# Sum of squares of an input tile in halves on ACT and DVE, and the softmax's maximum with its sign turned

## The chip, the core and the metric

The program runs on one core of a Trainium2 chip. The metric is the device time of one execution in microseconds; three executions of the kernel before gave 641.45, 641.72 and 641.73, a median of 641.72. The profile of a kernel is taken from one execution of its own. The engines are named as in the profile: PE multiplies matrices, PEld loads its weights, ACT applies functions, DVE is the vector engine, POOL the general engine, SP issues DMAs.

## The reference, cut to what matters

One layer of a decoder: a normalized input is projected, three groups of heads mix it (a recurrent one, one with block-sparse attention, a gated one), and a feed-forward block follows. The change touches the first normalization and the attention's softmax:

```python
def rmsnorm(x, g):                       # x: 512 tokens of 1024 channels
    y = x * lax.rsqrt(jnp.mean(x * x, axis=-1, keepdims=True) + 1e-6)
    return y * g
...
logits = einsum(q, k) * 0.125            # 6 heads of 64 channels, 512 tokens
p = softmax(where(mask, logits, -inf), axis=-1)
o = einsum(p, v)
```

## The kernel before

Tokens lie in four tiles of 128. `xt` holds the input as four tiles of 128 partitions (tokens) by 1024 channels. All matrix products use a split of each operand into a rounded high part and a low remainder (h and l in the names), so each product is three.

The first stage, up to about 25 us, has its order written out by hand on all five engines: what stands first in the program runs first on its engine. `norm_x(t)` takes the sum of squares of tile t on ACT (L265, with an accumulator output into `ss`), then forms the mean plus 1e-6 on POOL (L266) and its power of -1/2 on POOL (L267, into `rs`). For tiles 0 and 1 `diag_x` (L288, DVE) turns `rs` into a diagonal matrix by which PE turns and scales at once; for tiles 2 and 3 `scale_x` (L270, DVE) multiplies the tile and PE transposes it. `turn_x(th, k)` transposes channel block k of a pair of tiles on PE, and gives its high part on ACT (L281, `bigh`) and its low part on DVE (L282, `bigl`). `split` cuts the first weights: the high part on ACT (L296), the low part on POOL (L297). On DVE the order of the first stage is: diag of tile 0, the copy of the norm's gain `gcol` (L311), diag of tile 1, then the L282 of the channel blocks 0 to 7 and the two L270. `norm_x(2)` and `norm_x(3)` stand behind `turn_x(0, 5)` and `turn_x(0, 6)`. PE alternates between high and low products of a block as `turn_x` delivers it.

Behind this stage PE's order is still given by the program (the class `Order` interleaves side work by due times that are counted in PE's columns), while the order on ACT, DVE, POOL and SP is made by a planner that simulates the program and picks by priority what is ready. POOL's preparations (masks, constants) are such work, and the planner has put them ahead of the first L266.

The attention's `scores(qb)` has PE multiply queries `qs` and keys into a PSUM bank `s`, DVE take the maximum of a row (L845), DVE multiply it by -0.125 (L846), ACT take exp(0.125 s + that) with its sum (L848), DVE the reciprocal (L849) and the scaling of the row (L850). This happens 24 times, between 141 and 226 us. `turned(qb)` then transposes the row on PE (L117) and copies it on ACT (L859). `dense_qk` produces the queries: the high part of the product by a copy on ACT (L987), the low part by a difference on DVE (L989).

Of the kernel before, what the change touches and what calls it, by code (L numbers as in the profile page):

```python
# [8 lines left out]
F32 = mybir.dt.float32  # L9
F32R = mybir.dt.float32r  # L10
BF = mybir.dt.bfloat16
AF = mybir.ActivationFunctionType
OP = mybir.AluOpType
AX = mybir.AxisListType

S = 512
D = 1024
# [79 lines left out]
def block_kernel(ctx: ExitStack, tc: tile.TileContext, x, pre_mix_g, w_in, rwkv_mu, rwkv_w0, rwkv_w2,  # L97
# [4 lines left out]
    act, dve, pool, sp = nc.scalar, nc.vector, nc.gpsimd, nc.sync  # L102
# [34 lines left out]
    def sb():  # L137
        return bank("sb", 3)

    def ob():  # L140
        return bank("ob", 1)
# [4 lines left out]
    def ct(shape, name, dt=F32):  # L146
        return const.tile(shape, dt, name=name)
# [78 lines left out]
    ss = ct([128, 4], "ss")  # L226
    rs = ct([128, 4], "rs")
# [11 lines left out]
    xt = p0p.tile([128, NB, D], F32, name="xt")  # L239
    junk = p0p.tile([128, D], BF, name="junk")  # L240
    diag = p0p.tile([128, 2, 128], F32, name="diag")
    ET = mybir.EngineType
    with tc.manual_schedule(engines={ET.PE, ET.Activation, ET.DVE, ET.Pool, ET.SP}):
# [18 lines left out]
        pe.transpose(pc, grow0, ident[:KB, :KB])  # L262

        def norm_x(t):
            act.activation(junk, xt[:, t, :], AF.Square, scale=1.0 / 32, accum_out=ss[:, t:t + 1])  # L265
            pool.tensor_scalar(rs[:, t:t + 1], ss[:, t:t + 1], 1.0, 1e-6, op0=OP.mult, op1=OP.add)  # L266
            pool.tensor_tensor(rs[:, t:t + 1], rs[:, t:t + 1], mhalf[:, 0:1], op=OP.pow)  # L267

        def scale_x(t):
# [35 lines left out]
        def step(i, th, k):  # L305
            dense(i, th, wh, h1, k)
            dense(i, th, wh, l1, k)

        norm_x(0)
        diag_x(0)  # L310
        dve.tensor_copy(gcol, pc)  # L311
        norm_x(1)
        diag_x(1)
        split(0, 0, pool)
# [4 lines left out]
        for k in range(KB):  # L319
            dense(0, 0, wh, h1, k)  # L320
            if k == 0:
                split(1, 0, pool)
            if k == 2:
                split(1, 1, pool)
            if k < KB - 3:
                turn_x(0, k + 3)
            if k in (2, 3):
                norm_x(2 + (k > 2))
            if k in (4, 6):
                scale_x(k // 2)  # L330
            dense(0, 0, wh, l1, k)
            if k >= LAG:
                step(1, 0, k - LAG)
# [133 lines left out]
    def dense_fm(free=False):  # L467

        wh, wl = feed.next()
        wh = wh.rearrange("p (k c) -> p k c", k=KB)  # L470
        wl = wl.rearrange("p (k c) -> p k c", k=KB)
        p = acc()
        for k in range(KB):
            pe.matmul(p, wh[:, k], h1[:, k], start=(k == 0), stop=False)
            pe.matmul(p, wh[:, k], l1[:, k], start=False, stop=False)
            pe.matmul(p, wl[:, k], h1[:, k], start=False, stop=(k == KB - 1))
            if free:
                od.signal("free%d" % k)
            if k < KB - 1:
                od.pump()  # L480
        return p
# [28 lines left out]
    HR = [slice(0, 64), slice(64, 128)]  # L510
# [318 lines left out]
    def head(pair, hh):  # L829
        yield "qk%d" % pair  # L830
        yield "inverse"
        yield "vt"
        if pair:
            yield "att%d" % (pair - 1)
        a = 2 * pair + hh

        def scores(qb):
            n = 128 * qb + 128
            s = sb()
            qs, ks, kl = QK[pair]  # L840
            pe.matmul(s[:, :n], qs[:, hh, n - 128:n], ks[:, hh, :n], start=True, stop=False, skip_group_check=True)
            pe.matmul(s[:, :n], qs[:, hh, n - 128:n], kl[:, hh, :n], start=False, stop=False, skip_group_check=True)
            pe.matmul(s[:, n - 128:n], identb, negm, start=False, stop=True, skip_group_check=True)
            mx = att.tile([128, 4], F32, name="mx%d" % hh, bufs=2)
            dve.tensor_reduce(mx[:, 0:1], s[:, :n], axis=AX.X, op=OP.max)  # L845
            dve.tensor_scalar(mx[:, 1:2], mx[:, 0:1], -0.125, None, op0=OP.mult)  # L846
            e = st_["at2"].tile([128, S], F32, name="ee%d" % hh, bufs=2)
            act.activation(e[:, :n], s[:, :n], AF.Exp, bias=mx[:, 1:2], scale=0.125, accum_out=mx[:, 2:3])  # L848
            dve.reciprocal(mx[:, 3:4], mx[:, 2:3])  # L849
            dve.tensor_scalar(e[:, :n], e[:, :n], mx[:, 3:4], None, op0=OP.mult)  # L850
            return e

        def turned(qb, e):
            n = 128 * qb + 128
            pt = sb()
            for kb in range(qb + 1):
                pe.transpose(pt[:, 128 * kb:128 * kb + 128], e[:, 128 * kb:128 * kb + 128], ident)
            pts = st_["at2"].tile([128, NB, 128], F32, name="pts%d" % hh, bufs=2 - hh)
            act.copy(pts[:, :qb + 1, :], pt[:, :n].rearrange("p (k c) -> p k c", c=128))  # L859
            return pts  # L860

        def weighted(qb):

            n = 128 * qb + 128
            if pair not in pos:
                pos[pair] = ob()
            for kb in range(qb + 1):
                for h in range(2):
                    pe.matmul(pos[pair][HR[h], n - 128:n], vt[:, kb, pair, h, :], ptss[pair, h, qb][:, kb, :],
                              start=(qb == 0), stop=(kb == qb), skip_group_check=True)  # L870
            od.signal("sum%d_%d" % (pair, qb))

        yield 1500.0 * hh
        e = scores(0)
        due = od.t + T_SM + 2.4 * 128
        for qb in range(NB):
            yield due - od.t
            if not hh and qb > 1:
                yield "sum%d_%d" % (pair, qb - 2)
            ptss[pair, hh, qb] = turned(qb, e)  # L880
            t0 = od.t
            if qb < NB - 1:
                e = scores(qb + 1)
                due = od.t + T_SM + 2.4 * (128 * qb + 256)
            od.signal("pts%d_%d" % (a, qb), t0 + T_PT + 0.8 * (128 * qb + 128) - od.t)
            if hh:
                yield "pts%d_%d" % (a - 1, qb)
                yield "pts%d_%d" % (a, qb)
                weighted(qb)
        od.signal("head%d" % a)  # L890
# [90 lines left out]
    def dense_qk(b):  # L981

        qs, ks, kl = QK[b]
        p = dense_fm()
        with tc.high_priority(offset=PRI_W):
            for h in range(2):
                act.copy(qs[HR[h], h], p[HR[h]])  # L987
            for h in range(2):
                dve.tensor_tensor(qs[HR[1 - h], h], p[HR[h]], qs[HR[h], h].bitcast(F32), op=OP.subtract)  # L989
        od.pump()  # L990
        for h in range(2):
            pool.memset(kl[HR[1 - h], h].bitcast(F32), 0.0)
        p = dense_fm()
        with tc.high_priority(offset=PRI_W):
            for h in range(2):
                act.copy(ks[HR[h], h], p[HR[h]])
            for h in range(2):
                dve.tensor_tensor(kl[HR[h], h], p[HR[h]], ks[HR[h], h].bitcast(F32), op=OP.subtract)
        for h in range(2):
            pool.tensor_scalar(ks[HR[1 - h], h], ks[HR[h], h].bitcast(F32), 1.0, 0.0, op0=OP.mult, op1=OP.add)  # L1000
        od.pump()
        od.signal("qk%d" % b, T_QK)
# [8 lines left out]
    AO = [ca.rearrange("p a b -> p (a b)")[:, :S], ca.rearrange("p a b -> p (a b)")[:, S:],  # L1011
          ar[:, 0, 0:4].rearrange("p c a s -> p (c a s)")]
    dense_qk(0)
    dense_qk(1)
    dense_qk(2)
    p = dense_fm()
    shift(p, 10, sg)
# [21 lines left out]
    for b in range(2):  # L1039
        p = dense_fm(b == 1)  # L1040
# [574 lines left out]
```

## Time and profile before

| | us |
|---|---|
| median of three executions (lowest, highest) | 641.72 (641.45, 641.73) |
| the profiled execution's own time | 641.61 |
| its span in the trace | 639.9 |
| PE busy in the span | 623.0 |
| DVE busy | 490.1 |
| ACT busy | 327.7 |
| POOL busy | 56.8 |

The span is 1.7 us shorter than the execution's time; what lies around it is no part of the trace. Matrix products run one into the other, and a busy PE is not a PE at its peak; but an idle PE is time in which it waited.

### The profile page before, as it was taken

The page shows a single profiled execution, that of the slowest core. Times are in us where ns is not written, and L with a number is a line of the kernel's source. Part 1 is how long each engine was busy: PE and PEld are TensorE (multiplying, and loading weights), DVE is VectorE, ACT ScalarE, POOL GpSimd, SP SyncE. Part 2 cuts the span into 40 slices and gives each one's busy share as a digit, 9 for nine tenths or more (in the row PEclk, how much of TensorE's full clock was granted, in tenths as well). Part 3 has the DMA queues.
Part 4 walks back from the last instruction along what each step waited for, and adds up shares of the span by engine and source line. Part 5 has one row for each costly group of instructions (what it writes and reads, how often), then busy time and mean ns, then how long its engine had stood idle before and what let it go on. Part 6 is the DMA issues. An engine that isn't in the chain of part 4 may idle for free.

```text
span 639.9 us, 11545 instructions
## 1 busy us (share of the span) xinstructions
PE 623.0 (97%) x4582; PEld 548.6 (86%) x4582; DVE 490.1 (77%) x835; ACT 327.7 (51%) x582; POOL 56.8 (9%) x107
## 2 busy tenths in 40 slices
PE   7999999999999999999999999999999999999995
PEld 7877778877767887888999999999999988888884
DVE  2789969886575779558988888788897748979825
ACT  6653543365554464447755555555455434646511
POOL 7021111032130100011000000000000000000001
PEclk9999999999999999999999999999999999999999
DMA  7421111421211117315424333343333235775403
GB/s 233 125 64 50 57 50 61 129 69 47 59 34 34 35 40 289 122 44 155 139 73 130 99 107 101 92 131 99 100 104 96 67 122 198 256 232 182 160 0 132
DMA packets 84981, 69.12 MB, mean 108 GB/s; under 512 B 2968, under 2 KB 70976, under 8 KB 84928
## 3 DMA queue, kind: packets, MB, share of 16 engines
q1 hardware_dynamic: 83024, 65.76, 33.1%
q10 hardware_dynamic: 1904, 2.63, 1.4%
q8 instruction: 36, 0.59, 0.4%
q14 instruction: 17, 0.14, 0.1%
HBM read 66.28 MB, written 2.10 MB: 107 GB/s over the span
## 4 chain that ended last, share of the span: by engine, by line
PE 79%; DVE 4%; issue 1%; ACT 1%; POOL 0%; DVEq 0%; POOLq 0%; ACTq 0%
PE acc L112 34%; PE sb L112 30%; PE rb L112 5%; PE yb L112 5%; PE ob L112 3%; PE sb L117 2%; DVE wl L185 1%; DVE x L1566 1%; ACT wdad L1532 0%; DVE tinv L657 0%; PE rb L117 0%; PE yb L117 0%; DVE y L666 0%; POOL rs L1564 0%; DVE s L1556 0%
## 5 line engine op out<-in xcount | busy, mean ns | idle before, releaser
L112 PE MATMUL acc<-bigh,wh 128*128 128x512 f32 (+1 forms) x168 | 67.2, 403 | 0.3 <-ACT bigh L281 0.3
L112 PE MATMUL acc<-bigl,wh 128*128 128x512 f32 (+1 forms) x168 | 63.3, 381 | 0.3
L183 ACT ACTIVATE wh<-wf 128x512 fp32r<-128x512 f32 (+2 forms) x60 | 40.4, 711 | 44.2 <-PE acc L112 29.3
L112 PE MATMUL sb<-h,wh 128*128 128x256 f32 x260 | 61.4, 282 | 0.0
L112 PE MATMUL sb<-l,wh 128*128 128x256 f32 x260 | 61.4, 282 | 0.0
L185 DVE TENSOR_TENSOR wl<-wf,wh 128x512 fp32r<-128x512 f32 (+2 forms) x60 | 47.0, 805 | 17.5 <-ACT wh L183 15.4
L112 PE MATMUL acc<-bigh,wl 128*128 128x512 f32 (+1 forms) x168 | 59.0, 376 | 0.0
L1318 ACT ACTIVATE wh<-wf 128x1024 fp32r<-128x1024 f32 x38 | 39.9, 1058 | 30.6 <-DVE wf L1339 13.8
L1319 DVE TENSOR_TENSOR wl<-wf,wh 128x1024 fp32r<-128x1024 f32 x38 | 46.0, 1222 | 10.4 <-ACT wh L1318 10.3
L112 PEld LDWEIGHTS sb<-l,wh 128*128 128x128 f32 x260 | 47.5, 190 | 0.0
L112 PEld LDWEIGHTS sb<-h,wh 128*128 128x128 f32 x260 | 47.5, 190 | 0.0
L1411 ACT ACTIVATE wh<-wf 128x1024 fp32r<-128x1024 f32 x25 | 26.2, 1058 | 33.5 <-PE sb L112 23.4
L112 PE MATMUL sb<-h,wl 128*128 128x256 f32 x260 | 41.0, 282 | 0.0
L1412 DVE TENSOR_TENSOR wl<-wf,wh 128x1024 fp32r<-128x1024 f32 x25 | 30.1, 1220 | 10.6 <-ACT wh L1411 10.6
L112 PEld LDWEIGHTS acc<-bigh,wh 128*128 128x128 f32 x168 | 31.8, 189 | 7.0 <-issue 1.3
L112 PEld LDWEIGHTS acc<-bigl,wh 128*128 128x128 f32 x168 | 31.8, 189 | 5.6 <-DVE bigl L282 0.9
L1318 ACT ACTIVATE wh<-sums 128x1024 fp32r<-128x1024 f32 x19 | 20.1, 1061 | 30.3 <-PE acc L112 17.2
L112 PEld LDWEIGHTS sb<-h,wl 128*128 128x128 f32 x260 | 35.4, 191 | 0.0
L112 PEld LDWEIGHTS acc<-bigh,wl 128*128 128x128 f32 x168 | 29.8, 188 | 6.2
L1319 DVE TENSOR_TENSOR wl<-sums,wh 128x1024 fp32r<-128x1024 f32 x19 | 23.2, 1223 | 11.7 <-ACT wh L1318 11.7
L1564 POOL TENSOR_TENSOR rs<-rs,mhalf 128x1 f32<-128x1 f32 x4 | 2.2, 550 | 333.3 <-DVE rs L1559 329.9
L1357 DVE TENSOR_TENSOR frow<-sb,grow 128x512 f32<-128x512 f32 x19 | 13.1, 688 | 17.2 <-PE sb L112 17.2
(489 smaller groups left out, 1764.3 us busy)
## 6 DMA issues: line engine op xcount, KB each, us to landing
wf<-in_w_ffn_in_dram SPq DMA_DIRECT2D x76, 256.0 KB
wf<-in_w_ffn_out_dram SPq DMA_DIRECT2D x37, 512.0 KB
wf<-in_w_in_dram SPq DMA_DIRECT2D x21, 512.0 KB
wf<-in_w_out_dram SPq DMA_DIRECT2D x8, 512.0 KB
wf<-in_w_ffn_in_dram SPq DMA_DIRECT2D x6, 512.0 KB
xt<-in_x_dram SPq DMA_DIRECT2D x4, 512.0 KB
x<-in_x_dram SPq DMA_DIRECT2D x4, 512.0 KB
out_dram<-x SPq DMA_DIRECT2D x8, 256.0 KB
```

The lines of the kernel that those rows point to most:

```text
L112: return nc.tensor.matmul(out_, lhsT, rhs, **kw)
L117: return nc.tensor.transpose(out_, in_, idn)
L183: act.activation(h[:, c], t[:, c], AF.Copy)
L185: eng.tensor_tensor(l[:, c], t[:, c], h[:, c].bitcast(F32), op=OP.subtract)
L1318: act.activation(h, src, AF.Copy)
L1319: dve.tensor_tensor(l, src, h.bitcast(F32), op=OP.subtract)
L1357: dve.tensor_tensor(em[1], pc, su.rearrange("p i c -> p (i c)"), op=OP.add)
L1411: act.activation(h, src, AF.Copy)
L1412: dve.tensor_tensor(l, src, h.bitcast(F32), op=OP.subtract)
L1564: pool.tensor_tensor(r, r, mhalf[:, 0:1], op=OP.pow)
L1566: dve.scalar_tensor_tensor(x2[:, t, c], src, r, x2[:, t, c], op0=OP.mult, op1=OP.add)
```

## The change

Each of the four L265 takes 512 of the 1024 channels on ACT; the other 512 are squared and summed on DVE by one instruction with an accumulator output (the mean's factor 1/1024 goes into it), and a second DVE instruction on one column adds the two halves and 1e-6. POOL's L266 goes; L267 stays. In the softmax the maximum is taken with its sign turned by the same instruction, L846 goes, and the factor 0.125 moves from the exponential into both parts of the queries.

```diff
         def norm_x(t):
-            act.activation(junk, xt[:, t, :], AF.Square, scale=1.0 / 32, accum_out=ss[:, t:t + 1])
-            pool.tensor_scalar(rs[:, t:t + 1], ss[:, t:t + 1], 1.0, 1e-6, op0=OP.mult, op1=OP.add)
+            act.activation(junk[:, 0:512], xt[:, t, 0:512], AF.Square, scale=1.0 / 32, accum_out=ss[:, t:t + 1])
+            dve.scalar_tensor_tensor(junk[:, 512:], xt[:, t, 512:], 1.0 / D, xt[:, t, 512:], op0=OP.mult, op1=OP.mult,
+                                     accum_out=rs[:, t:t + 1])
+            dve.scalar_tensor_tensor(rs[:, t:t + 1], ss[:, t:t + 1], 1e-6, rs[:, t:t + 1], op0=OP.add, op1=OP.add)
             pool.tensor_tensor(rs[:, t:t + 1], rs[:, t:t + 1], mhalf[:, 0:1], op=OP.pow)
...
-            dve.tensor_reduce(mx[:, 0:1], s[:, :n], axis=AX.X, op=OP.max)
-            dve.tensor_scalar(mx[:, 1:2], mx[:, 0:1], -0.125, None, op0=OP.mult)
+            dve.tensor_reduce(mx[:, 1:2], s[:, :n], axis=AX.X, op=OP.max, negate=True)
             e = st_["at2"].tile([128, S], F32, name="ee%d" % hh, bufs=2)
-            act.activation(e[:, :n], s[:, :n], AF.Exp, bias=mx[:, 1:2], scale=0.125, accum_out=mx[:, 2:3])
+            act.activation(e[:, :n], s[:, :n], AF.Exp, bias=mx[:, 1:2], accum_out=mx[:, 2:3])
...
             for h in range(2):
-                act.copy(qs[HR[h], h], p[HR[h]])
+                act.activation(qs[HR[h], h], p[HR[h]], AF.Copy, scale=0.125)
             for h in range(2):
-                dve.tensor_tensor(qs[HR[1 - h], h], p[HR[h]], qs[HR[h], h].bitcast(F32), op=OP.subtract)
+                dve.scalar_tensor_tensor(qs[HR[1 - h], h], p[HR[h]], 0.125, qs[HR[h], h].bitcast(F32),
+                                         op0=OP.mult, op1=OP.subtract)
```

## Rows read from the trace of the kernel before

**Rows 1.** Stretches: us, then busy us (instructions) of PE, PEld, DVE, ACT, POOL; clock, DMA

```profile
17.00:30.00 13.00, 12.98 (x95) 11.87 (x95) 9.19 (x22) 8.63 (x17) 0.89 (x6) 1.00 0.37 104
141.00:225.00 84.00, 81.51 (x886) 63.33 (x881) 53.49 (x155) 43.56 (x118) 14.44 (x18) 1.00 0.15 42
```

**Rows 2.** Timeline, 4 to 9 us: start, duration, instruction, [idle before <-releaser]

```profile
4.70 1.06 ACT L265 ACTIVATE junk<-xt 128x1024 bf16<-128x1024 f32 x1 [1.77 <-DMA xt<-in_x_dram]
4.87 0.29 POOL L461 TENSOR_SCALAR_AFFINE_SELECT tri<-tri 128x128 f32<-128x128 f32 x1
5.62 0.46 POOL L456 TENSOR_TENSOR cbd<-cbd,ident 128x128 f32<-128x128 f32 x1
5.66 0.19 ACT L265 ACTIVATION_READ_ACCUMULATOR junk<-xt 128x1 f32 x1
6.06 1.06 ACT L265 ACTIVATE junk<-xt 128x1024 bf16<-128x1024 f32 x1 [0.21 <-DMA xt<-in_x_dram]
6.44 0.56 POOL L267 TENSOR_TENSOR rs<-rs,mhalf 128x1 f32<-128x1 f32 x1
6.46 0.22 PE L117 MATMUL ob<-ident,grow 8*128 8x8 f32 x1
7.03 0.29 DVE L288 TENSOR_SCALAR diag<-ident,rs 128x128 f32<-128x128 f32 x1 [7.03 <-POOL rs L267]
7.24 0.16 DVE L311 COPY gcol<-ob 128x8 f32<-128x8 f32 x1
8.16 0.29 DVE L288 TENSOR_SCALAR diag<-ident,rs 128x128 f32<-128x128 f32 x1 [0.77 <-POOL rs L267]
```

**Rows 3.** Timeline, 10 to 17 us

```profile
10.54 3.77 POOL L297 TENSOR_TENSOR wl<-wf,wh 128x512 fp32r<-128x512 f32 x3 [0.73 <-ACT wh L296]
13.00 0.48 DVE L282 SCALAR_TENSOR_TENSOR bigl<-sb,gcol,bigh 128x256 fp32r<-128x256 f32 x1 [0.38 <-ACT bigh L281]
15.80 0.48 DVE L282 SCALAR_TENSOR_TENSOR bigl<-sb,gcol,bigh 128x256 fp32r<-128x256 f32 x1 [0.92 <-ACT bigh L281]
16.34 0.19 PEld L112 LDWEIGHTS acc<-bigl,wh 128*128 128x128 f32 x1 [0.33 <-DVE bigl L282]
```

**Rows 4.** PE's waits from 130 to 245 us: total us, times, longest

```profile
PE sb L117 <- DVE ee L850: 1.6, 1, 1.6
PE sb L117 <- ACT ee L848: 0.4, 1, 0.4
```

**Rows 5.** Groups by line and shape: busy us, mean ns of one | idle before

```profile
L571 DVE SCALAR_TENSOR_TENSOR kn<-kn,en 128x512 f32<-128x512 f32 x3 | 2.1, 688 | 0.1
L296 ACT ACTIVATE wh<-wf 128x512 fp32r<-128x512 f32 x4 | 2.5, 631 | 0.6 <-DMA wf<-in_w_in_dram 0.6
```

**Rows 6.** One sum and the power behind it, 622 us, timeline

```profile
622.24 0.15 DVE L1559 SCALAR_TENSOR_TENSOR rs<-sm 128x1 f32<-128x1 f32 x1
622.47 0.55 POOL L1564 TENSOR_TENSOR rs<-rs,mhalf 128x1 f32<-128x1 f32 x1 [322.45 <-DVE rs L1559]
```

**Rows 7.** DVE beside POOL: timeline rows; durations of L1158, min/median/max ns

```profile
51.23 1.29 DVE L185 TENSOR_TENSOR wl<-wf,wh 128x512 fp32r<-128x512 f32 x2
180.78 1.43 POOL L742 TENSOR_TENSOR rsb<-sv,pcc 64x192 f32<-64x192 f32 x2 [2.12 <-DVE sv L761]
181.12 1.63 DVE L185 TENSOR_TENSOR wl<-wf,wh 128x512 fp32r<-128x512 f32 x2
L1158 POOL TENSOR_TENSOR rs<-rs,mhalf x4: 550/554/1462, 274.2 to 294.1; 128x1 f32<-128x1 f32 x4
```

**Rows 8.** Timeline of two softmaxes, 184 to 208 us

```profile
184.67 0.16 DVE L849 RECIPROCAL mx<-mx 128x1 f32<-128x1 f32 x1
206.39 0.28 DVE L845 TENSOR_REDUCE mx<-sb 128x1 f32<-128x128 f32 x1
206.99 0.14 DVE L846 TENSOR_SCALAR mx<-mx 128x1 f32<-128x1 f32 x1
207.16 0.37 ACT L848 ACTIVATE ee<-sb,mx 128x128 f32<-128x128 f32 x1 [0.55 <-DVE mx L846]
```

## The prediction, made before the changed kernel was seen

> **What bounds the kernel now.** I read the table of stretches first, to see in which stages PE stands idle at all, then PE's waits, to see for whom, and then the timeline of those places. From 17 to 30 us PE is busy for 12.98 of 13 us [rows 1], and over the whole span for 623.0 of 639.9 us (the table above): what PE loses or gains early it carries to the end, because its order is fixed and little idle time lies behind to take up a shift. The two halves of the change touch two places where PE does wait. The first is the start: until tile 1 has its diagonal matrix (8.16 us [rows 2]) PE has almost nothing to do, and from 14 to 17 us it is held up by the last low parts of the blocks: its load at 16.34 waits for the L282 that began at 15.80 [rows 3]. The second is the attention, where PE idles 2.5 of 84 us [rows 1]. Two waits of PE there name the softmax, of 1.6 and 0.4 us [rows 4]. So the most that the second half can return is about 2 us, and the start can be worth 1 or 2 us either way. I carry everything against the profiled execution, 641.61 us, which lies 0.11 below the median 641.72.
>
> **The start, tile 0.** Half of the squares on ACT takes about 0.63 us by the 128x512 L296 [rows 5] instead of 1.06, and the accumulator read of 0.19 begins 0.1 before the end [rows 2]: from 4.70 it ends at 5.42. The DVE half is a two-tensor instruction of 128x512 on SBUF: 0.69 by L571 [rows 5], and the sum behind it 0.15 by L1559 [rows 6]. The trace has no accumulator output on DVE; its extra time, r, lies between nothing and ACT's 0.19 [rows 2]; I take 0.07, because a small DVE instruction overlaps the one ahead by about 0.08 (L311 starts 0.08 before the diagonal's end [rows 2]). The sum is at hand at 5.65, and with the hop of 0.08 from such a sum to a power (622.39 to 622.47 [rows 6]) POOL could begin its power at 5.73 instead of 6.44. But POOL's queue has preparations ahead of it: from L461 at 4.87 to the end of L456 at 6.08 [rows 2], 1.21 us of them. And they read SBUF while the DVE half reads two operands from SBUF (4.70 to 5.39). Such neighbours hold each other up: two L185 take 1.63 us beside the two L742, otherwise 1.29, and one L1158 took 1462 ns instead of 554 [rows 7]. So L461 waits for up to 0.52; I take 0.4, as both rows show most of such an overlap as waiting and not all of it. POOL is then free at 6.48, and the power runs from 6.56 to 7.12: the diagonal of tile 0 comes at 7.15 instead of 7.03.
>
> **The start, tile 1.** This is the step on which I put most weight. DVE works in order, and the half of tile 1 stands behind diag 0 and the copy of gcol. The tile is there at 6.06 [rows 2], but DVE is waiting in diag 0 for POOL. The copy follows at 7.36 (0.21 behind, as now), the half of tile 1 begins at 7.44 and ends at 8.13; then 0.04 of hand-over, r and 0.15 for the sum: 8.39; hop, power of 0.56, 0.03: the diagonal of tile 1 starts at 9.06 instead of 8.16, 0.90 later. So the halves of tile 1 do not run at the same time, and ACT's is done long before it is wanted. Bounds: if the planner puts the power ahead of the preparations, diag 0 comes at 6.32, the copy must still wait for PE's turned gain (6.46 plus 0.22 [rows 2]), the half begins at 6.81, and without r diag 1 comes at 8.36, 0.20 later. With the full 0.52 and r of 0.19 it is 9.30, 1.14 later.
>
> **The start, tiles 2 and 3.** Here ACT gains about 0.43 us twice, and the high parts come sooner; but the low parts decide. Counted as if nothing before had moved: DVE begins L282 of block 5 at 13.00 [rows 3] and is free for the half of tile 2 at 13.40. The last L297 of POOL (three of them from 10.54 to 14.31, 1.26 each, so from 13.05 [rows 3]) streams two operands until 14.31. The wait of DVE lies between 0 and 0.91; I take 0.6. The pair of L185 lost 0.34 in about 1.1 us of such company, which would be 0.3 here; L1158 waited almost to the end of its neighbour, which would be the whole [rows 7]. The half then ends at 14.69, its sum runs from 14.80 to 14.95, L282 of block 6 from 14.87, the half of tile 3 from 15.27 to 15.96, its sum from 16.07 to 16.22, and L282 of block 7 starts at 16.14 instead of 15.80: 0.34 later. Without wait and r it starts at 15.40 (0.40 sooner), with 0.91 and r of 0.19 at 16.69 (0.89 later). All blocks move with diag 1, so PE leaves this stage 0.90 + 0.34 = 1.24 us later; between 0.20 - 0.40 = -0.20 and 1.14 + 0.89 = 2.03. POOL's L266 saves nothing that is left over: it was replaced by the sum on DVE with one more hop. The scalings L270 follow the last L282 as now and move with it.
>
> The Trainium skill (SBUF — State Buffer, § Who interferes with whom) says that a DVE instruction with two SBUF inputs contends with a GpSimd instruction that reads SBUF, and that the later one is blocked until the other has finished. The rows of L1158 and of the L185 pair agree in kind; by that rule alone the wait of tile 2 would be the whole 0.91, and the stage 0.3 us later than I sum it.
>
> **The attention.** 24 L846 of about 0.15 us leave DVE, but DVE is not the bound there, with 53.49 of 84 us busy [rows 1]. What counts is where the exponential waits and PE waits for it. At 206.39 the maximum takes 0.28, then another instruction stands ahead of L846 (206.99), and the exponential begins at 207.16 [rows 8]; it could begin at about 206.72, 0.44 sooner. PE's wait of 0.4 for that bank [rows 4] goes: -0.43 by the two timeline rows. The wait of 1.6 does not go by itself: its row scaling follows the reciprocal at 184.67 [rows 8], which stands in DVE's queue behind weight splits and keys, and no L846 but one lies between, within the usual distance of reciprocal and scaling. Turning the sign in the reduction I cost at nothing, since the instruction reads the same elements; the same holds for the factor in the queries' copy and difference, 6 each, which keep their operands' sizes. If they cost 0.15 each (a whole small instruction by L1559 [rows 6]) they would lie beside PE work, at worst 12 times 0.15 = 1.8 us in total off the path; if the sign cost as much as L846 did, the 0.43 would be lost. So this part lies between -2.0 (both waits gone) and 0; I take -0.43.
>
> **Sum.** +1.24 - 0.43 = +0.81; 641.61 + 0.81 = 642.4, by the median 642.5. A difference of 0.2%, 1.28 us, is about what a measurement of this kernel can tell from no change; so I forecast no change that can be told, leaning to slower. The parts' bounds give -2.2 to +2.0.
>
> **Rivals.**
> 1. *The start costs nothing*: POOL takes the power ahead of its preparations and the ports do not collide. Then -0.20 - 0.43: 641.1. For it: the sum is ready 0.2 us before L266 was. Against it: the last preparation begins at 5.62, before 5.73 [rows 2].
> 2. *The planner re-orders the attention and the long wait goes too*: with the maximum ready 0.2 sooner the exponential gets ahead of the weight splits on ACT. With a start of about +0.5 that is +0.5 - 0.43 - 1.6 = -1.5: 640.2. For it: that order is made from simulated times, and every one of the 24 chains changes. Against it: the splits have the higher priority.
> 3. *Slower, by the DVE instruction itself*: an accumulating two-tensor instruction runs at half speed. Each half then costs more by between 0.5 and its whole 0.69 us, I take 0.6; halves 1, 2 and 3 lie on the path, +1.8: 644.3. It decides as soon as the half lasts longer than about 0.9 us. Against it: L571 with two SBUF operands takes 0.69 [rows 5]; but it has no accumulator. The Trainium skill (Vector Engine (DVE) Microarchitecture Reference, § Points that are easy to get wrong) says that this form with two non-bf16 SBUF sources halves its throughput; L571 does not show that, and no row here has the accumulator with it.
> 4. *Slower, by a new order*: the planner puts a softmax instruction behind splits once more, with a wait like the longest now, 1.6 us: 644.1.
>
> **Chances.** The forecast 0.55 (its own range 641.3 to 643.8; a quarter of it lies above 643.0), rival 1 0.13, rival 2 0.17 (two thirds of it below 640.4), rival 3 0.07, rival 4 0.08. Slower by over 0.2%: 0.14 + 0.07 + 0.08 = 0.29; faster 0.12; the rest, 0.59, within. The range 640.6 to 644.0 leaves out most of rival 2, rival 3 and the tail of rival 4.
>
> **What would show it.** In the changed profile: the DVE half of tile 1 starts after gcol, not at 6.06, and diag 1 starts near 9.0; the half of tile 2 lasts longer than the half of tile 1; PE's load for block 7 comes near 17.6; PE's wait near 207 for the exponential is gone. I am wrong if diag 1 comes before 8.4, if the half of tile 1 lasts over 0.9 us, or if PE's idle time between 141 and 226 us changes by more than 1 us either way.

## The result and the profile after

The changed kernel took 645.89 us in the median of four executions (644.89 to 647.59), the kernel before 641.65 beside it (641.45 to 641.73): a ratio of 1.0058, 95% interval 1.0038 to 1.0078. It is slower, by more than the range of the prediction allowed. Measured again, beside 21 executions of the kernel before on one chip, it was 645.07 against 642.60, 1.0036 (1.0023 to 1.0048). Executions of one kernel can lie 4 us apart or more (641.3 to 645.4 for the kernel before, 643.0 to 649.5 for e3 below), so each ratio below is taken to the kernel before on the same chip. The profiled execution of the changed kernel took 645.79 us, with a span of 644.1.

What was foreseen on VectorE is there to the hundredth, and next to it what was not. The timeline of the changed kernel from 4 to 11 us (it answers [rows 2]):

```profile
4.84 0.69 DVE L266 SCALAR_TENSOR_TENSOR junk<-xt 128x512 bf16<-128x512 f32 x1 [4.84 <-DMA xt<-in_x_dram]
4.89 0.80 POOL L463 TENSOR_SCALAR_AFFINE_SELECT tri<-tri 128x128 f32<-128x128 f32 x1
...
7.15 0.29 DVE L290 TENSOR_SCALAR diag<-ident,rs 128x128 f32<-128x128 f32 x1 [1.33 <-POOL rs L269]
7.35 0.16 DVE L313 COPY gcol<-ob 128x8 f32<-128x8 f32 x1
7.43 0.68 DVE L266 SCALAR_TENSOR_TENSOR junk<-xt 128x512 bf16<-128x512 f32 x1
...
8.03 0.63 ACT L298 ACTIVATE wh<-wf 128x512 fp32r<-128x512 f32 x1 [1.02 <-DMA wf<-in_w_in_dram]
8.04 0.08 DVE L266 DVE_READ_ACCUMULATOR junk<-xt 128x1 f32 x1
8.22 0.16 DVE L268 SCALAR_TENSOR_TENSOR rs<-ss,rs 128x1 f32<-128x1 f32 x1
8.46 0.56 POOL L269 TENSOR_TENSOR rs<-rs,mhalf 128x1 f32<-128x1 f32 x1 [1.34 <-DMA prow<-in_rwkv_k_a_dram]
8.98 1.26 POOL L299 TENSOR_TENSOR wl<-wf,wh 128x512 fp32r<-128x512 f32 x1
9.05 1.28 DVE L290 TENSOR_SCALAR diag<-ident,rs 128x128 f32<-128x128 f32 x1 [0.67 <-POOL rs L269]
...
10.38 0.58 PE L112 MATMUL sb<-diag,xt 128*128 128x128 f32 x1 [2.40 <-DVE diag L290]
```

The half of tile 1 stands behind the copy of the gains at 7.43, its diagonal starts at 9.05. But POOL's low part of the first weights (L299, the L297 of before) begins 0.07 us ahead of that diagonal, and the diagonal takes 1.28 us instead of its usual 0.29. In the kernel before, the diagonal started at 8.16 [rows 2] and the low part at 8.54, after it:

```profile
8.50 1.38 PE L112 MATMUL sb<-diag,xt 128*128 128x128 f32 x10 [0.64 <-DVE diag L288]
8.54 1.27 POOL L297 TENSOR_TENSOR wl<-wf,wh 128x512 fp32r<-128x512 f32 x1 [0.42 <-ACT wh L296]
```

PE starts its first product of tile 1 at 10.38, 1.88 later than the 8.50 of the kernel before.

The next view is the table of stretches for PE: us, busy us (instructions), granted clock, DMA share, GB/s.

```profile
7.00:8.00 1.00, 0.49 (x2) 1.00 1.16 290
8.00:9.00 1.00, 0.00 (x0) 0.87 1.18 333
9.00:10.00 1.00, 0.00 (x0) 0.50 1.01 395
10.00:12.00 2.00, 1.62 (x7) 0.50 0.64 247
12.00:14.00 2.00, 2.00 (x12) 0.50 0.00 1
14.00:16.00 2.00, 2.00 (x13) 0.61 0.15 44
16.00:18.00 2.00, 2.00 (x20) 1.00 0.74 218
```

PE does nothing from about 8 us until 10.38. In that pause the granted clock falls from 1.00 (2.4 GHz) to 0.50 (1.2 GHz), and it is back only between 15 and 16 us: PE's first 5 us of real work run at half speed. So the load for block 7, at 16.34 before [rows 3], comes at 20.17.

The attention, the same view with all engines (busy of PE, PEld, DVE, ACT, POOL; it answers the second of [rows 1]) and PE's waits from 130 to 245 us (total us, times, longest; [rows 4]):

```profile
141.00:225.00 84.00, 83.05 (x967) 64.36 (x960) 52.47 (x130) 44.76 (x120) 15.04 (x20) 1.00 0.16 46
```

```profile
PE sb L117 <- DVE ee L851: 0.4, 1, 0.4
PE sb L112 <- ACT pts L860: 0.4, 1, 0.4
PE ob L112 <- ACT pts L860: 0.2, 1, 0.2
```

PE's idle time there goes from 2.5 to 0.95 us. The wait of 1.6 is 0.4, the one of 0.4 for the exponential is gone, one of 0.2 is new: 1.4 less. (The wait of 0.4 for L860 is not new: it is there before too, for L859.) On the timeline the long wait shrinks because the planner chose another order. In the kernel before, the exponential stood behind two copies of keys (`ks`) on ACT, and the scaling behind two key differences (`kl`) on DVE:

```profile
180.73 1.17 ACT L996 CAST ks<-acc 64x512 fp32r<-64x512 f32 x2
181.93 0.47 ACT L848 ACTIVATE ee<-sb,mx 128x256 f32<-128x256 f32 x1
183.26 1.38 DVE L998 TENSOR_TENSOR kl<-acc,ks 64x512 fp32r<-64x512 f32 x2
184.87 0.35 DVE L850 TENSOR_SCALAR ee<-ee,mx 128x256 f32<-128x256 f32 x1
```

In the changed kernel both are ahead of the keys:

```profile
185.15 0.47 ACT L849 ACTIVATE ee<-sb,mx 128x256 f32<-128x256 f32 x1
185.59 1.18 ACT L998 CAST ks<-acc 64x512 fp32r<-64x512 f32 x2
...
187.09 0.15 DVE L850 RECIPROCAL mx<-mx 128x1 f32<-128x1 f32 x1
187.75 0.74 DVE L851 TENSOR_SCALAR ee<-ee,mx 128x256 f32<-128x256 f32 x1
188.42 1.38 DVE L1000 TENSOR_TENSOR kl<-acc,ks 64x512 fp32r<-64x512 f32 x2
```

It is the order that counts, and not the 0.15 us of L846: the maximum of this row was ready over 1 us ahead of its exponential in both kernels (at 179.70 for 181.93, and at 183.94 for 185.15). The 0.4 that is left fits a neighbour on POOL again, though no run tried it: the scaling of this row takes 0.74 instead of 0.35, beside a POOL instruction on `ks` (L1002) that runs from 186.71 to 188.35.

Last, PE's waits from 500 us to the end. The kernel before has none there in its profiled execution:

```profile
PE acc L112 <- DVE wl L1414: 1.5, 1, 1.5
```

To see where a shift arises I follow three markers through every kernel: the start of the first time shift (L235), the start of the addition of `lnb` (L926 of before, behind the attention), and the start of the first final addition (L1554 of before). The kernel before has them at 26.8, 246.4 and 620.1 us. The table gives, in us of one profiled execution each, the start's shift (first marker against before), what changes from the first to the second marker, and what changes from the second to the third. Since executions differ, a row can differ from its kernel's median.

| kernel | start | attention | last stages |
|---|---|---|---|
| changed kernel | +3.9 | -1.3 | +1.6 |
| e1, sums of squares alone | +2.5 | +0.1 | 0.0 |
| e2, softmax alone | +1.9 | -1.4 | +0.7 |
| e3, before with a later start | +1.4 | 0.0 | +1.7 |
| e4, changed, PE kept busy | +2.4 | -1.4 | +0.5 |
| e5, changed, low part held | +1.9 | -1.4 | +1.1 |
| e6, changed, halves ahead | +0.5 | -1.4 | +1.5 |
| e7, as e6, two tiles only | +0.4 | -1.3 | +3.7 |
| e8, as e7, PE kept busy | +0.4 | -1.3 | -0.2 |
| e9, before, fewer loads | -0.1 | 0.0 | -0.2 |
| e10, changed, fewer loads | +3.6 | -1.3 | -0.2 |
| e11, softmax alone, PE kept busy | 0.0 | -1.4 | -0.1 |
| e12, changed kernel again | +3.6 | -1.3 | +1.3 |

The attention's column goes with the softmax half of the change and with nothing else. The start's column goes with the order, the pauses and the clock there. The last column goes with neither; the runs below take it apart.

### The profile page after: what moved, and what is told of

Its sections match the earlier page's. It is cut to its first block, busy times and chain, and to the rows that moved or that the text cites. A ratio compares the mean times of both kernels' runs of the same rounds, so it can differ in the third digit from the quotient of the medians.

```text
span 644.1 us, 11518 instructions
## 1 busy us (share of the span) xinstructions
PE 625.0 (97%) x4582; PEld 550.8 (86%) x4582; DVE 492.2 (76%) x823; ACT 326.2 (51%) x582; POOL 56.7 (9%) x103
## 4 chain that ended last, share of the span: by engine, by line
PE 74%; DVE 6%; DMA 2%; ACT 2%; issue 2%; POOL 0%; DVEq 0%; POOLq 0%; ACTq 0%
PE acc L112 31%; PE sb L112 28%; PE rb L112 5%; PE yb L112 4%; PE ob L112 3%; DMA wf<-in_w_ffn_out_dram 2%; PE sb L117 2%; DVE wl L1414 1%; DVE wl L185 1%; DVE x L1568 1%; DVE sw L1459 0%; ACT wdad L1534 0%; ACT wh L1413 0%; DVE tinv L659 0%; PE rb L117 0%
## 5 line engine op out<-in xcount | busy, mean ns | idle before, releaser
L185 DVE TENSOR_TENSOR wl<-wf,wh 128x512 fp32r<-128x512 f32 (+2 forms) x60 | 46.9, 805 | 18.0 <-ACT wh L183 17.6
L1414 DVE TENSOR_TENSOR wl<-wf,wh 128x1024 fp32r<-128x1024 f32 x25 | 30.1, 1221 | 10.9 <-ACT wh L1413 10.9
L1320 ACT ACTIVATE wh<-sums 128x1024 fp32r<-128x1024 f32 x19 | 20.2, 1061 | 30.2 <-PE acc L112 17.2
```

The lines of the kernel that those rows point to most:

```text
L185: eng.tensor_tensor(l[:, c], t[:, c], h[:, c].bitcast(F32), op=OP.subtract)
L1320: act.activation(h, src, AF.Copy)
L1414: dve.tensor_tensor(l, src, h.bitcast(F32), op=OP.subtract)
```

## The experiments

### e1 and e2: each half alone

e1 is the kernel before with the new `norm_x`, e2 the kernel before with the new softmax and queries; their edits are the first and the last two pieces of the change's diff.

> The kernel before with the change of the input tiles' sums alone; the softmax is as before. In the profile of the changed kernel everything up to the attention comes 3.9 us later than before, the attention gives back 1.4 us, and the last matrix stage (transfers of w_ffn_out) loses 1.6 us again. Theory A (the loss is made in the first stage, and the two halves of the change add up): PE's load for block 7 comes near 20.2 us instead of 16.34, the last row scaling of the attention 3.9 us later than before, and the time is 645.5 us, or up to 647 if the last stage stalls here too. Rival B (the later softmax order is what moves the start's loss on): the shift shrinks before the attention, and the time is under 644. If the last stage's stall belongs to the softmax's new order, it is missing here.

> The kernel before with the change of the softmax alone; the input tiles' sums are as before. Theory A: the start is as before, PE's wait of 1.6 us for a scaled row in the attention shrinks to about 0.4 us and the 0.4 us wait for the exponential goes, and the time is 640.3 us (1.4 less than before). Rival: the gain in the attention only exists because the shifted start changed what is ready when; then the attention's waits are as before and the time is 641.3 to 641.7. If the stall in the last stage belongs to the softmax's order, PE waits there for 1 us or more and the time is 641 to 642.

Measured: e1 646.63 us, ratio 1.0058 (1.0040 to 1.0077); e2 641.59, ratio 0.9983 (0.9970 to 0.9996). So the halves of the change pull in opposite directions. Both missed an expectation. e1's profiled execution is its fastest (644.12) and has PE's load for block 7 at 18.78, not near 20.2: the diagonal of tile 1 lasts 1.28 there too, but the clock falls only after 11 us and is back at 15, and the half of tile 2 meets no neighbour (0.71). e2's median lies 1.0 below the kernel before and not 1.4; only its three fastest executions (640.24 to 640.39) reach what was expected. PE's waits from 130 to 245 us in e1:

```profile
PE sb L117 <- DVE ee L852: 1.6, 1, 1.6
PE sb L117 <- ACT ee L850: 0.4, 1, 0.4
```

and in e2:

```profile
PE sb L117 <- DVE ee L849: 0.4, 1, 0.4
```

The re-ordering comes with the softmax alone, so the rival of e2 falls, though the median lies in its range. Which part of the softmax's change moved the planner (the multiplication that is gone, or the factor in the queries) was not tried by itself. e2's profiled execution was above its median (642.77), with a wait of 0.7 in the last stages and a late start. In the start, tile 1 landed 0.7 us later than in the kernel before, which has the same order there; the stretches of PE:

```profile
7.00:8.00 1.00, 0.64 (x4) 1.00 1.17 292
8.00:9.00 1.00, 0.00 (x0) 1.00 1.18 324
9.00:10.00 1.00, 0.82 (x6) 0.92 1.02 391
10.00:13.00 3.00, 3.00 (x16) 0.50 0.46 181
13.00:14.00 1.00, 1.00 (x10) 0.88 0.01 2
```

With PE's wait for that diagonal at 1.3 us instead of 0.64, the clock fell here too, in the order of the kernel before; but it fell 0.6 us after PE had taken up its work again at 9.18. So the order of the kernel before can run into the low clock by itself, when a tile lands late.

### e3 and e4: a shift without the change, the change without the low clock

```diff
 # e3, on the kernel before
-N_WARM = 24
+N_WARM = 51
```

```diff
 # e4, in turn_x of the changed kernel; warm is a tile that nobody reads
+                if not th and not k and t:
+                    for _ in range(12):
+                        pe.transpose(warm[:, 0:128], ident, ident)
                 if th:
                     pe.transpose(pt[:, c], xk, ident)
```

> The kernel before with 51 instead of 24 warming transposes ahead of PE's first stage, and nothing else: PE is kept busy and its first product starts about 3.8 us later, with no half on DVE and no pause of PE. Theory A (a delay at the start goes through to the end one for one): 645.4 us, clock 1.00 throughout, and the first stage itself as long as before. If the stall of the last stage comes from the mere moment at which the transfers of w_ffn_out run, it shows here too: PE waits there 1 us or more, 646 to 647.5 us, with runs that differ by more than 1 us. Rival (slack behind the start takes up part of a delay): under 644.5.

> The changed kernel with 12 transposes of the identity put between PE's first two turned tiles, so that PE works while it waits for tile 1's diagonal. Theory A (the granted clock fell to 0.50 from about 8.7 to 15.6 us because PE stood idle from 8.0 to 10.4, and that costs 1 to 1.5 us): the clock stays at 1.00, PE's load for block 7 comes at 18.6 to 19.2 instead of 20.2, and the time is 1.0 to 1.5 us under the changed kernel's, 644.4 to 644.9. Rival (the low clock costs nothing, since DVE's low parts set the stage's end): load for block 7 stays at 20 us, time 645.9.

Measured: e3 643.95 us, 1.0029 (1.0003 to 1.0054); e4 643.74, 1.0019 (1.0006 to 1.0033). The 27 added transposes of e3 ran at about 0.11 us each, 3.0 us in all, and part of that went into time in which PE had waited for the diagonals, so the start moved by 1.4 us only and not by 3.8. That 1.4 arrives behind the attention undiminished (table): up to there a shift of the start is paid in full. The medians differ by 1.36, though with an interval of 0.2 to 3.5 us. e3's profiled execution also has 1.7 us in the last stages, without any part of the change.

In e4 the diagonal of tile 1 is as long as in the changed kernel, and PE starts its product of tile 1 at 10.29, 1.79 later than before. But its clock stays:

```profile
8.00:9.00 1.00, 1.00 (x11) 1.00 1.17 332
9.00:10.00 1.00, 0.16 (x2) 1.00 1.03 401
10.00:13.00 3.00, 2.71 (x24) 1.00 0.42 162
```

and the start's shift is 2.4 instead of 3.9, with the load for block 7 at 18.65 as expected; the rival, which had it at 20, falls (the time came out under the 644.4 to 644.9 that were expected). The low clock costs the changed kernel the other 1.5 us, in the profiled execution. In that of e12, the same kernel, the clock is low only from about 11.3 to 14.8 instead of 8.7 to 15.6, PE's first product of tile 1 comes later (10.71), and the start's shift is 3.6: the sum is much the same, its parts are not.

### e5: the neighbour of the diagonal

POOL's first low part is held by a one-column operation that reads block 0 of the turned input. The calls (the switch inside `split` and the tile `hold` are left out here):

```diff
-        split(0, 0, pool)
-        for k in range(2):
-            turn_x(0, k)
+        split(0, 0, pool, False)          # the high part alone
+        turn_x(0, 0)
+        pool.tensor_scalar(hold, h1[:, 0, 0:1].bitcast(F32), 1.0, 0.0, op0=OP.mult, op1=OP.add)
+        split(0, 0, pool, None)           # the low part alone
+        turn_x(0, 1)
```

> The changed kernel with one thing more: POOL's first low part of the weights (L299, 1.26 us, which started 0.07 us ahead of the diagonal of tile 1) is held back by a one-column POOL operation that reads channel block 0 of the turned input; nothing is left out. Theory (that neighbour is what stretched the diagonal from 0.29 to 1.28 us): the diagonal starts near 9.05 again but lasts 0.29, the first product of tile 1 starts near 9.4 instead of 10.38, and the shift at the end of the start is 1 us less than the changed kernel's +3.9, more if the granted clock then stays at 1.00. The low part comes some 1.5 us later, which the products with the high parts cover. Time 644.5 to 645.0, or near 643.5 if the clock holds. Rival (the diagonal was long for a reason of its own, such as the accumulator reads on VectorE): it stays near 1.28 and the time stays near 645.9.

Measured: 643.28 us, 1.0018 (1.0007 to 1.0030). Timeline from 8 to 14 us:

```profile
8.78 0.55 POOL L270 TENSOR_TENSOR rs<-rs,mhalf 128x1 f32<-128x1 f32 x1 [1.90 <-DVE rs L269]
9.37 0.29 DVE L291 TENSOR_SCALAR diag<-ident,rs 128x128 f32<-128x128 f32 x1 [0.67 <-POOL rs L270]
9.71 1.38 PE L112 MATMUL sb<-diag,xt 128*128 128x128 f32 x10 [1.54 <-DVE diag L291]
...
10.95 3.78 POOL L303 TENSOR_TENSOR wl<-wf,wh 128x512 fp32r<-128x512 f32 x3
```

Without the neighbour the diagonal lasts 0.29, although both accumulator reads still stand ahead of it on VectorE. So the neighbour was the cause, and the rival falls. The diagonal starts at 9.37 and not at 9.05, because here the transposed gains came 1 us later (7.36 against 6.40) and with them the copy and the half of tile 1; the same happened in e10 and e12, which do not have this edit. The clock held through a pause of 1.54 us:

```profile
8.00:9.00 1.00, 0.17 (x2) 1.00 1.19 325
9.00:10.00 1.00, 0.29 (x2) 1.00 1.00 393
10.00:13.00 3.00, 3.00 (x29) 1.00 0.45 176
```

Beside e2, where it fell behind a pause of 1.3 us, this says that the length of one pause alone does not decide; what else does is not settled here.

### e6, e7 and e8: the halves of tile 1 in a better place

e6 exchanges two steps of VectorE's order; e7 does the same but leaves tiles 2 and 3 in the form of the kernel before; e8 is e7 with 8 transposes as in e4.

```diff
         norm_x(0)
+        norm_x(1)
         diag_x(0)
         dve.tensor_copy(gcol, pc)
-        norm_x(1)
         diag_x(1)
```

> The changed kernel with two steps exchanged on VectorE: the half and the sum of tile 1 stand ahead of the diagonal of tile 0 and the copy of the gains; nothing is left out. Theory (the loss comes from tile 1's half standing behind the diagonal of tile 0 and from what follows from that, PE's pause and the low clock): tile 1's half runs at 6.2 to 6.9, its power near 7.15, its diagonal near 7.8, PE's product of tile 1 starts near 8.1, ahead of the 8.50 of the kernel before; the clock stays at 1.00. What is left is the half of tile 2 beside POOL's low part (0.42 us long), so that the start's shift is between -0.4 and +0.5, and with the attention's -1.4 the time is 639.8 to 641.0. Rival (halves on VectorE cost by themselves, wherever they stand, by slowing POOL and the copies of the start): the shift at the end of the start stays above +2 and the time above 643.

> As the run with the halves first, but tiles 2 and 3, whose sums nobody waits for early, keep the form of the kernel before (the whole square on ScalarE, mean and power on POOL); the softmax is the changed one, nothing is left out. Theory: the diagonal of tile 1 near 7.8, no half of tile 2 in VectorE's way, shift of the start -0.4 to 0, attention -1.4: 639.8 to 640.3. Rival (as above, the halves cost by themselves): above 642.

> The run before with 8 transposes of the identity, written to a tile that nobody reads, between the first two turned tiles on PE, which fill the pause until the diagonal of tile 1. Theory (when the input's tiles come late, PE's pause lets the granted clock fall to 0.50 for some 5 us, which is part of why single executions of one kernel differ by several us): same fastest time as the run before within 0.5 us, clock at 1.00 from 6 to 17 us in the profile, and executions that lie closer together. Rival (the scatter comes from transfers of the last stage alone): the spread stays as it is, and the transposes cost 0 to 0.4 us.

Measured: e6 642.00 us, 0.9994 (0.9981 to 1.0007); e7 640.92, 0.9987 (0.9972 to 1.0003); e8 640.69, 0.9978 (0.9967 to 0.9989). In e6 the half of tile 1 runs while DVE had been waiting, and its diagonal is early and short:

```profile
5.92 1.01 POOL L458 TENSOR_TENSOR cbd<-cbd,ident 128x128 f32<-128x128 f32 x1
5.92 0.69 DVE L266 SCALAR_TENSOR_TENSOR junk<-xt 128x512 bf16<-128x512 f32 x1 [0.32 <-DMA xt<-in_x_dram]
...
8.00 0.29 DVE L290 TENSOR_SCALAR diag<-ident,rs 128x128 f32<-128x128 f32 x1 [0.16 <-POOL rs L269]
8.44 1.27 POOL L299 TENSOR_TENSOR wl<-wf,wh 128x512 fp32r<-128x512 f32 x1 [0.47 <-ACT wh L298]
...
13.23 1.47 DVE L266 SCALAR_TENSOR_TENSOR junk<-xt 128x512 bf16<-128x512 f32 x1
```

The start's shift is +0.5 instead of +3.9: one exchange takes back 3.4 us, so the halves do not cost by themselves wherever they stand. The half of tile 1 now holds up a preparation on POOL instead (L458, 1.01 for 0.45), and the diagonal still comes 0.16 earlier than in the kernel before. What is left is the half of tile 2 beside POOL's low part (1.47 instead of 0.69). e6's time missed its expectation (639.8 to 641.0): its median is that of the kernel before, where the table's start and attention alone would give 0.9 less, and its profiled execution has 1.5 in the last stages. e7, without that half, gains only 0.1 us in its start, since there the first weights landed later (their high part starts at 8.94). e7 missed its expectation of 639.8 to 640.3 by 0.6, and its profiled execution, at 644.36, had the long wait of the last stage, in which the clock fell as well (stretch of PE):

```profile
560.00:570.00 10.00, 8.14 (x29) 0.83 0.63 193
```

In e8 nine of eleven executions lie between 640.44 and 640.86, and its profile has no wait for low parts after 500 us; the clock is 1.00 from 6 to 17 us as expected, and the start is no earlier than e7's. The executions of e11 below, with the same transposes, lie as close (640.05 to 640.54); those of e4, with 12 of them, do not (642.89 to 645.67). The expectation had a mechanism for part of this, a start whose clock no longer falls, as it did in e2; how the transposes at 8 us should quiet a wait between 560 and 570 us is not shown, and may be chance of the transfers.

### e9, e10 and e12: the last stage

```diff
             a, x = w2_load(ka, 512), b12
-            other = w2_load(kb, 512)
-            dve.tensor_tensor(sw, a, other, op=OP.add)
+            dve.tensor_tensor(sw, a, a, op=OP.add)
```

e9 has this edit on the kernel before, e10 on the changed kernel: both leave out three weight tiles and so a part of the computation. e12 is the changed kernel itself again.

> The kernel before without the second weight tiles of the product p5 in the last stage (three tiles of 512 KB are not read, the sum takes the first tile twice): this leaves out part of the computation, and takes transfers out of the stretch in which PE waited for low parts of weights. Theory (the last stage's wait of 0 to 1.9 us is weights that land late, and it comes and goes from one execution to the next of any kernel): PE has no wait for low parts after 530, the median comes down to the fastest executions of the kernel before, 641.0 to 641.6, and the executions lie closer together. Rival (the wait comes from a shifted start, not from transfers): no change against the kernel before in median or spread.

> The changed kernel with the same three tiles not read. Theory (of the 4.2 us that the changed kernel lost, the start and the attention together make +2.5 and the late weights 1.6): no wait for low parts after 530, and 2.5 us (2.0 to 3.0) more than the kernel before with the same three tiles left out. Rival (the last stage loses time for a reason of the change itself): still 3.5 to 4.2 us more.

> The changed kernel as it is, beside the others on one chip and with more executions. Theory (start +3.9, attention -1.4, late weights 0 to 1.9): executions from 2.5 to 4.4 us above the fastest of the kernel before, 643.8 to 646, median 644.5 to 645.5. Rival (it loses 4.2 us each time): all executions within 0.5 us of 645.9.

Measured on one chip, where the kernel before had 642.60 (641.28 to 645.05): e9 641.50 (641.47 to 642.99), e10 643.83 (642.73 to 643.90), e12 645.07 (644.28 to 645.35). Neither e9 nor e10 has a wait of PE after 500 us; the stretch that held 1.5 us of it in the changed kernel is full in e10:

```profile
560.00:570.00 10.00, 10.00 (x45) 1.00 0.60 209
```

while e12 has it again, at 1.2 us, for the same L1414. So that wait goes with the loads: weights land too late for their split. With three tiles less to load it is in neither profile, and the executions of the kernel before lie closer (641.47 to 642.99); those of the changed kernel spread over 1.1 to 1.2 us with and without the loads. Two of e9's eleven still lie 1.5 us above the rest, at a lower mean clock (0.993 against 0.996 to 0.998), so these three loads are not the only source of scatter. The change costs 643.83 - 641.50 = 2.33 us, which fits +3.6 - 1.3 of e10's row. e12's 2.47 above the kernel before says the same with the loads in place.

### e11: the best of the parts

The softmax change alone, with the 8 transposes of e8 and the sums of squares of the kernel before.

> The kernel before with the softmax change alone and 8 transposes of the identity, written to a tile that nobody reads, between the first two turned tiles; nothing left out. It tells what the halves of tiles 0 and 1 are worth beside the run that had them in the better order with the same transposes (640.69 in its median). Theory (PE's start is bound by the arrival of tiles and weights once the clock holds): within 0.5 us of that run, the diagonal of tile 1 near 8.2 and the first shift at 27.0 to 27.4. Rival (halves in the right order bring the start forward): that run is faster by 0.5 us or more.

Measured: 640.31 us (640.05 to 640.54), 0.9964 (0.9951 to 0.9976). It beats the kernel before by 0.36%, and the changed kernel by more. Its start is that of the kernel before (shift 0.0, the first marker at 26.8 where 27.0 to 27.4 was expected) with the clock at 1.00, its attention 1.4 us shorter. e2, the same without the transposes, had 0.9983, and its fastest execution (640.24) is as fast: what the transposes seem to take away is slow executions, but the two intervals touch. e8, with the halves of tiles 0 and 1 in their better place, starts 0.4 later, and its ratio of 0.9978 is no better; the two ran on different chips, but nothing in either profile shows the halves to be worth anything here.

## Why the prediction was wrong

It gave 642.5 with a range of 640.6 to 644.0, and slower by over 0.2% a chance of 0.29. Point by point:

- **Tile 0 and the order on DVE: right.** The half lasts 0.69, r is 0.08 (0.07 taken), POOL's L463 was held up to 0.80 from 0.29 (0.51 of the 0.64 that it ran beside the half; 0.4 taken, with a bound of 0.52), diagonal 0 starts at 7.15 and the half of tile 1 at 7.43 (7.44). That it fits to the hundredth is in part luck: the preparations ended 0.11 later than summed, and the power followed them without the hop of 0.08. And the reason given for 0.4 was misread: the L185 pair lost 0.34 of 1.1, which is not most of it; only L1158 lost most.
- **Diagonal of tile 1: its start right, its length wrong.** 9.05 against 9.06. The first step that failed is that the diagonal was priced at 0.29 wherever it stands, though all rows of such neighbours [rows 7] were on the table and were used for POOL's preparations and for tile 2. Moved 0.9 us later, it meets POOL's next instruction. POOL's queue holds the low part right behind the power; before, the low part had to wait for its high part until 8.54, which is past 8.16. Now the high part is done (8.03 + 0.63 = 8.66) by the time the power ends, at 9.02, and that lets both the low part and the diagonal go, POOL first. That is +0.99 by the row, there in all five profiles with this order (1.27 or 1.28 in the changed kernel, e1, e4, e10 and e12) and gone in e5.
- **No term for PE's pause: the second step that failed.** The sum let PE leave the stage as late as its last operand. It read the clock as 1.00 [rows 1] in stretches without pauses, and did not ask what a pause of 2.4 us does to it. e4 shows 1.5 us. The load for block 7, foreseen near 17.6, came at 20.17.
- **Tiles 2 and 3: the kind right, the size about right.** In the changed kernel the half of tile 2 waited 0.42 (0.6 taken), for less of the neighbour was left to meet; in e6, where little had moved, 0.78. PE's load for block 7 came there 0.36 later than before (16.70 against 16.34) with the diagonal 0.16 earlier, 0.52 in all, where the sum had 0.34.
- **The attention: -0.43 foreseen, -1.3 to -1.4 measured.** Rival 2 named the mechanism, at 0.17: the planner re-orders, and the long wait goes. Its argument against, that the splits have the higher priority, was beside the point: what the exponential passed were the key copies. The one-step timeline gain of 0.43 was right for its own wait (0.4, gone). Of the signs of being wrong this one showed: PE's idle time from 141 to 225 us changed by more than 1 us, for the better.
- **The last stage.** That weights can land late there, for 0 to 1.9 us in one execution or another, was in no term, and no row of the kernel before showed it. In the first comparison it stood on the changed kernel's side (1.6 of the 4.2 us in the profile), in the second it stood on both.
- **Rival 3 is refuted**: the halves of tiles 0, 1 and 3 take 0.68 to 0.69 with an accumulator and two SBUF operands, as L571 without one [rows 5], and that of tile 2 takes 1.11 only beside POOL (0.71 in e1, with no neighbour). The Trainium skill (Vector Engine (DVE) Microarchitecture Reference, § Points that are easy to get wrong) expects that halving; the trace does not agree.

Worked out with the measured terms of the profiled execution: start 0.89 + 0.99 + 1.5 + about 0.5 (what is left for tiles 2 and 3) = 3.9; attention -1.4; together +2.5, or 644.1 on the scale of the profiled execution of before. The rest to 645.79 is the late weights. Of what the change itself does, every miss that made it slower sat in the start, and the gain that I had sized too small hid a part of them: without the late weights the change costs 2.3 us (e10 against e9) where +0.8 was forecast. That such a cost would lie at the upper end of the range and not far past it is luck: two misses ran against each other.

What stays open: why the weights of the last stage land late in some executions, and what besides a pause's length lets the clock fall.

## What to carry to other kernels

When a step moves later, read what each queue will be doing at its new time, POOL's above all: a VectorE instruction priced from a quiet place can be held for nearly the whole of a neighbour that starts 0.07 us ahead of it. A wait of PE can have two prices, its length and the clock behind it; here 12 transposes into an unread tile bought off the second. And where a planner orders the queues, a small edit can be worth more through the new order than by its own time, so run such an edit alone.

## What the runs showed of the hardware

- A diagonal that reads one SBUF operand (a tensor_scalar of 128x128) was held by a POOL instruction that had started 0.06 to 0.07 us earlier: 1.27 or 1.28 us instead of 0.29, in the changed kernel, e1, e4, e10 and e12. In the changed kernel it ended 0.09 us behind that neighbour. The Trainium skill (SBUF — State Buffer, § Who interferes with whom) says that such a one-operand form can contend with GpSimd as well, under conditions, and that whoever issues first blocks the other; the rows agree in kind. The diagonal lost 0.99 of the 1.19 us that its neighbour had left, and tile 2's half in e6 lost 0.78 of 0.93, so most of the overlap but not all of it is lost.
- A DVE instruction with accumulator output is followed by a read of its own, 0.08 us by its row (8.04 in the changed kernel), against ACT's 0.19 [rows 2].
- The granted clock fell to 0.50 in PE's pause of 2.4 us (changed kernel), fell only after PE was at work again behind pauses of 2.4 (e1), 2.7 (e10), 2.5 (e12) and 1.3 us (e2), and stayed at 1.00 through one of 1.54 us (e5). Where it fell, PE worked several us at half speed before it rose.
